# Seven projections of a three-stage transformer block: 512 moving columns in place of 256

## The chip, the cores and the metric

The kernel is one program on one core of one Trainium2 chip. The metric is device time in microseconds of that program, as a median of several executions. One execution was taken by the hardware profiler; all rows below come from it.

## The reference

512 tokens of width 1024 go through two blocks. The first one mixes a gated linear recurrence with a spatial gating unit; the second pools, attends to the 128 best keys of each query, attends to 256 memory tokens and ends in 32 experts. All is float32.

```python
# first block
h = rmsnorm(x, norm_w);  proj = h @ w_in           # ten groups of 1024 columns
y_a = hgrn2(q, f_fwd, f_bwd, i, g)                 # chunks of 64 tokens, both directions
v = layernorm(gelu(v_raw))                         # v_raw = h @ (one group of w_in)
y_b = gelu(u) * mix(w_s, v) * silu(g_b)
x = rmsnorm(x + (sigmoid(m_a) * (y_a @ w_proj_a) + sigmoid(m_b) * (y_b @ w_proj_b)) @ w_out)
# second block
u = rmsnorm(x) @ w_in_2                            # pool, q, k, v, qi (512 each), ki, wi
score[t, s] = sum_h wi[t, h] * relu(qi[t, h] . ki[s]);  sel = top_k(score, 128)
att = softmax(rmsnorm(q) . rmsnorm(k)[sel]) @ v[sel]        # 8 heads of 64, rotary
x = x + concat(pool(u), att) @ w_out_2
q = rmsnorm(rmsnorm(x) @ xattn_wq);  x = x + memory_attention(q) @ xattn_wo   # 4 heads of 128
x = x + moe(rmsnorm(x))                            # 4 groups of 8 experts, width 256
```

## The kernel before

Each float32 product is made of three products in a shorter format: both operands are split into a high part and a low rest, and `mm3` (lines 160 to 163) adds high by high, high by low and low by high in one PSUM bank. Weights come through `load_w` (145 to 158): it loads a matrix block as two raw pieces of 512 KB on SyncE's queue (tag `wr`, two buffers), ScalarE copies the high part (139), and VectorE, or GpSimd where `eng` says so, subtracts for the low part (140). The two parts go into a buffer of the tag `w16`, of which there are two, or into a place given as `dst`.

Two shapes of product are used. With the weights stationary, 512 tokens move (`proj_T`), or with other weights of 512 columns the tokens are stationary. For the seven matrices of this change the tokens are stationary too (`proj_tok`), 128 at a time, and 256 columns of the weight move: a block of 256 columns with its whole contraction of 1024 fills one `w16` buffer, and a PSUM bank of 512 columns holds two token tiles side by side. The seven are the gating unit's value (`wv`, `pv`, in `sg_input`), the first output projection (`wo`, `pwo`, 631 to 648; `load_w4` puts half of its columns in `w16` and half in `wo_H`, `wo_L`), the index queries, keys and queries (`qk_unit`; `pqi`, `pk`, `pq`), the values (`v_unit`, `pvv`), the second output projection (`mix_out`, `pwo2`, in the trace under `pwo` too), and the cross attention's queries (`xq_unit`, `pxq`).

PSUM banks have three tags: `mm` (three banks, all projections), `sm` (three: scores and other small products) and `tp` (two: transposes). `head_norm` (544) normalises each head of a tile: ScalarE squares it out of PSUM, VectorE sums, GpSimd takes the power, VectorE multiplies, again out of PSUM; then `rotate` turns it on VectorE and GpSimd, and TensorE transposes it (`turn`).

`score(i)` (773 to 787) makes the index scores of token tile i: eight products on TensorE (780), a relu on ScalarE (782), a weighted sum on VectorE (784, 786). `topk(i)` (790 to 796) is sixteen rounds of two VectorE instructions on one tile's scores (794, 795). Lists of closures (`pend`, `turns`) and generators decide in which sequence pieces are written; a tile scheduler then sets each engine's sequence, from its own model of time. The expert layer at the end loads 1 MB pieces of gate and up weights on SyncE (1026) into a few buffers.

## Time and profile before

| | us |
|---|---|
| median of three runs | 1312.06 |
| lowest and highest of them | 1311.56, 1314.36 |
| profiled execution, own time | 1309.88 |
| its span on the core | 1308.1 |
| TensorE busy | 1263.4 |
| VectorE, ScalarE, GpSimd busy | 711.3, 490.3, 234.0 |

The mean granted clock of TensorE was 0.997 of full speed. Busy times of matmuls overlap with each other: a row lists a matmul from its start to its modelled end, and the next one starts before that. To see how many fit into a stretch one reads the starts.

### The profile page before, as it was taken

Reading aid. Unit: us, or ns where it says so; the run is one execution under the profiler, and the core shown is the slowest. Engines: PE = TensorE matmul, PEld = TensorE weight load, DVE = VectorE, ACT = ScalarE, POOL = GpSimd, SP = SyncE. Lnnn points to the kernel's source line nnn. Section 1 sums busy time; section 2 is a strip of 40 time slices with the busy share of each in tenths; the row PEclk is TensorE's granted clock in tenths of the full one; section 3 lists DMA queues with packets and bytes.
Section 4 is the critical chain, followed back from the end, with each engine's and each line's share of the span. In section 5 each row is a group of like instructions: output and inputs, shape, how many; then the busy total and the mean of one; then the engine's idle time right before and its main releaser. Section 6 shows DMA issues by size and latency. Waiting matters only on the chain.

```text
span 1308.1 us, 20715 instructions
## 1 busy us (share of the span) xinstructions
PE 1263.4 (97%) x8406; PEld 1000.3 (76%) x8406; DVE 711.3 (54%) x1299; ACT 490.3 (37%) x859; POOL 234.0 (18%) x278
## 2 busy tenths in 40 slices
...
GB/s 191 97 83 53 92 66 66 83 70 75 113 258 95 67 128 94 71 94 98 207 172 106 100 49 73 65 69 146 65 243 336 162 266 416 419 418 418 419 414 226
DMA packets 118085, 218.62 MB, mean 167 GB/s; under 512 B 15280, under 2 KB 94896, under 8 KB 106849
## 3 DMA queue, kind: packets, MB, share of 16 engines
...
## 4 chain that ended last, share of the span: by engine, by line
PE 83%; DVE 6%; DMA 6%; ACT 2%; issue 1%; POOL 1%; ACTq 0%; DVEq 0%; POOLq 0%
PE pgu L1368 8%; PE pl L327 2%; PE pf L162 2%; PE pwo L161 2%; PE pf L163 2%; PE pdn L1392 2%; PE pwo L162 2%; PE pf L161 2%; PE pwo L163 2%; DMA gu<-in_expert_w_gate 2%; PE pdn L1409 1%; PE pq L163 1%; PE ps L780 1%; DMA gu<-in_expert_w_up 1%; PE pq L161 1%; PE pq L162 1%
## 5 line engine op out<-in xcount | busy, mean ns | idle before, releaser
L1368 PE MATMUL pgu<-gu,hgT 128*64 128x512 f32 x512 | 119.0, 595 | 3.7 <-DMA gu<-in_expert_w_up 2.2
L1368 PEld LDWEIGHTS pgu<-gu,hgT 128*64 128x64 f32 x512 | 39.8, 137 | 71.7 <-issue 66.4
L361 ACT ACTIVATE qk<-G 128x512 f32<-128x512 f32 x112 | 69.1, 665 | 51.6 <-DVE G L351 51.6
L1373 DVE SCALAR_TENSOR_TENSOR sh<-sh,grs,pgu 128x256 f32<-128x256 f32 x16 | 7.7, 480 | 105.4 <-ACT sh L1372 105.4
L1372 ACT ACTIVATE sh<-pgu,grs 128x256 f32<-128x256 f32 x16 | 7.6, 474 | 139.2 <-PE pgu L1368 139.2
L348 DVE TENSOR_TENSOR G<-G,T 128x512 f32<-128x512 f32 x56 | 39.2, 701 | 31.4 <-ACT qk L361 28.6
L312 POOL TENSOR_TENSOR T<-T 128x512 f32<-128x512 f32 (+6 forms) x56 | 37.0, 660 | 42.6 <-DVE T L279 38.8
L1343 POOL DMA_INDIRECT hg<-x3d,srci x15 | 15.4, 1025 | 157.5 <-PE thg L1352 109.4
L161 PE MATMUL pi<-wi,hT_h 128*128 128x256 f32 x128 | 37.8, 296 | 3.3 <-ACT wi L139 1.8
L351 DVE TENSOR_TENSOR G<-G,T 128x512 f32<-128x512 f32 x56 | 38.8, 694 | 0.0
L162 PE MATMUL pi<-wi,hT_h 128*128 128x256 f32 x128 | 37.7, 294 | 0.0
L1392 PE MATMUL pdn<-dn,sh 128*64 128x512 f32 x160 | 37.4, 601 | 0.1
L163 PE MATMUL pi<-wi,hT_l 128*128 128x256 f32 x128 | 37.3, 291 | 0.0
L161 PE MATMUL pv<-wv,hT_h 128*128 128x256 f32 x128 | 36.8, 288 | 0.0
L163 PE MATMUL pv<-wv,hT_l 128*128 128x256 f32 x128 | 36.7, 286 | 0.0
L162 PE MATMUL pv<-wv,hT_h 128*128 128x256 f32 x128 | 36.5, 286 | 0.0
L162 PE MATMUL pg<-wga,hT_h 128*128 128x256 f32 x128 | 36.5, 285 | 0.0
L161 PE MATMUL pg<-wga,hT_h 128*128 128x256 f32 x128 | 36.4, 285 | 0.0
L163 PE MATMUL pg<-wga,hT_l 128*128 128x256 f32 x128 | 36.2, 283 | 0.0
L132 POOL TENSOR_SCALAR nm_r<-nm_q 128x1 f32<-128x1 f32 x2 | 2.5, 1254 | 182.5 <-ACT nm_s L200 182.4
L327 PE MATMUL pl<-qk 128*64 128x64 f32 x896 | 34.3, 225 | 0.0
L327 PEld LDWEIGHTS pl<-qk 128*64 128x64 f32 x896 | 29.3, 137 | 6.2 <-issue 2.1
...
## 6 DMA issues: line engine op xcount, KB each, us to landing
...
wo_r<-in_w_out SPq DMA_DIRECT2D x16, 512.0 KB, 3.6
wq_r<-in_w_in SPq DMA_DIRECT2D x12, 512.0 KB, 4.3
dn<-in_expert_w_down SPq DMA_DIRECT2D x10, 512.0 KB, 18.1
wi_r<-in_w_in SPq DMA_DIRECT2D x8, 512.0 KB, 6.5
wfb_r<-in_w_in SPq DMA_DIRECT2D x8, 512.0 KB, 4.3
```

What stands on the lines that cost most here:

```text
L161: nc.tensor.matmul(o, ah, bh, start=first, stop=False)
L162: nc.tensor.matmul(o, ah, bl, start=False, stop=False)
L163: nc.tensor.matmul(o, al, bh, start=False, stop=last)
L312: nc.gpsimd.tensor_tensor(ap_of(T, o, [[n2, 2], [1, n2]]), ap_of(T, a, [[sa, 2], [2, n2]]), ap_of(T, a + 1, [[sa, 2], [2, n2]]), OP.mult)
L327: nc.tensor.matmul(p[64 * j:64 * j + 64, c * 64:c * 64 + 64], kt[:, k0:k0 + 64], qt[:, q0:q0 + 64], start=True, stop=True)
L348: nc.vector.tensor_tensor(ap_of(G, 0, [[512, 2], [2 * m, nb], [1, m]]), ap_of(G, 0, [[512, 2], [2 * m, nb], [1, m]]), ap_of(T, a + 1, [[sa ...
L351: nc.vector.tensor_tensor(ap_of(G, 1024 + m, [[512, 2], [2 * m, nb], [1, m]]), ap_of(G, 1024 + m, [[512, 2], [2 * m, nb], [1, m]]), ap_of( ...
L361: nc.scalar.activation(ap_of(qk, a * 512, [[2 * m, nb], [m, 2], [1, m]]), ap_of(G, a * 512, [[2 * m, nb], [1024 + m, 2], [1, m]]), AF.Copy)
L780: nc.tensor.matmul(p[:, :n], qiT[hs, h // 2, i * 128:(i + 1) * 128], kiT[hs, :n], start=True, stop=True)
L1343: nc.gpsimd.indirect_dma_start(out=h, out_offset=None, in_=x3d, in_offset=bass.IndirectOffsetOnAxis(ap=sidx, axis=0), bounds_check=S - 1, ...
L1368: nc.tensor.matmul(pg[m * a:m * a + m, :], hT_[:, k, m * a:m * a + m], ap_of(gu, k * 256, [[2048, 2], [1, 256]]), start=k == 0, stop=k == 7)
L1392: nc.tensor.matmul(po[m * a:m * a + m, :], hd[:, f, m * a:m * a + m], dn[f][:, hs], start=f == 0, stop=f == 1)
```

## The change

`load_h` loads 512 columns as two halves of the contraction, each in a `w16` buffer of its own (named a and b), so that a raw piece is two blocks of 128 rows by 512 columns and a matrix takes both buffers. `proj_pair` takes two token tiles, a bank each: both with half a, then both with half b, so that every matmul has 512 moving columns. Evictions, residual adds and rotations are 512 wide for one token tile, where they were 256 wide for two. For keys, queries and cross queries `head_norm` first copies the bank to SBUF on ScalarE; the square and the multiply then read the copy. All key projections are written ahead of most score products, and `mix_out` gives way after each token tile and half. In all, 2112 matmuls of 256 columns become 1056 of 512; the other matmuls and the transposes keep their number.

```diff
+    def load_h(src, c0, name, eng=None, dst=(None, None)):
+        return [load_w(src[b * 512:(b + 1) * 512, :], c0, 512, f"{name}{'ab'[b]}", kb=4, eng=eng, dst=dst[b])
+                for b in range(2)]
...
+    def proj_half(o, acts, i, w, b):
+        a, k0 = (acts, 4 * b) if len(acts) == 2 and not isinstance(acts[0], tuple) else (acts[b], 0)
+        for k in range(4):
+            ts = slice(i * 128, (i + 1) * 128)
+            mm3(o, a[0][:, k0 + k, ts], a[1][:, k0 + k, ts], w[b][0][:, k, :], w[b][1][:, k, :],
+                b == 0 and k == 0, b == 1 and k == 3)
+    def proj_pair(acts, ip, w, name, between=None):
+        ps2 = [pmm(f"{name}_{2 * ip + ii}") for ii in range(2)]
+        for b in range(2):
+            for ii in range(2):
+                proj_half(ps2[ii], acts, 2 * ip + ii, w, b)
+            if b == 0 and between:
+                between()
+        return ps2
...
-        for c in range(4):
-            w = load_w(w_in, 6 * D + c * 256, 256, f"wv{c}")
+        for c in range(2):
+            w = load_h(w_in, 6 * D + c * 512, f"wv{c}")
             for ip in range(2):
-                p = pmm(f"pv{c}_{ip}")
-                for ii in range(2):
-                    proj_tok(p[:, ii * 256:(ii + 1) * 256], hT, 2 * ip + ii, w, 0, 256, range(8))
-                nc.scalar.activation(vn[:, 2 * ip:2 * ip + 2, c * 256:(c + 1) * 256],
-                                     p.rearrange("p (i c) -> p i c", i=2), AF.Gelu_apprx_tanh)
+                for ii, p in enumerate(proj_pair(hT, ip, w, f"pv{c}")):
+                    nc.scalar.activation(vn[:, 2 * ip + ii, c * 512:(c + 1) * 512], p, AF.Gelu_apprx_tanh)
...
-    def head_norm(p, name, nh, hd):
+    def head_norm(p, name, nh, hd, copy=False):
 
         t = s4(name)
+        if copy:
+            nc.scalar.activation(t[:, 1, :], p, AF.Copy)
+            p = t[:, 1, :]
...
-        ws = [load_w(src, c * 256, 256, f"{name}{c}", eng=eng) for c in range(2)]
+        first = load_h(src, 0, name, eng=eng)
         hi, lo = a16(name + "_H", F32R), a16(name + "_L", F32R)
-        for c in range(2):
-            ws.append(load_w(src, 512 + c * 256, 256, f"{name}{2 + c}",
-                             dst=(hi[:, :, c * 256:(c + 1) * 256], lo[:, :, c * 256:(c + 1) * 256]), eng=eng))
-        return ws
+        return [first, load_h(src, 512, f"{name}x", eng=eng,
+                              dst=[(hi[:, 4 * b:4 * b + 4, :], lo[:, 4 * b:4 * b + 4, :]) for b in range(2)])]
...
-            for c in range(4):
-                p = pmm(f"pwo{c}_{ip}")
-                for ii in range(2):
-                    proj_tok(p[:, ii * 256:(ii + 1) * 256], mT, 2 * ip + ii, wo[c], 0, 256, range(8))
-                for ii in range(2):
-                    residual(2 * ip + ii, c, 256, p[:, ii * 256:(ii + 1) * 256], xt[ii])
+            for c in range(2):
+                for ii, p in enumerate(proj_pair(mT, ip, wo[c], f"pwo{c}")):
+                    residual(2 * ip + ii, c, 512, p, xt[ii])
...
-                    for c in range(2):
-                        proj_tok(p[:, c * 256:(c + 1) * 256], mT, 2 * ip + ii, wo[2 * c2 + c], 0, 256, range(8))
+                    for b in range(2):
+                        proj_half(p, mT, 2 * ip + ii, wo[c2], b)
...
+    def qk_pair(w, ip, name, tab, norm, dst):
+        for ii, p in enumerate(proj_pair(h2T, ip, w, f"p{name}")):
+            i = 2 * ip + ii
+            if norm:
+                x = head_norm(p, f"{name}n{i}", 8, 64, True)
+            else:
+                x = s4(f"{name}x{i}")
+                nc.scalar.activation(x[:, 1, :], p, AF.Copy)
+            ro = rotate(x, tab, i, 1, 8, f"{name}o{i}", None)
+            def turn(i=i, ro=ro):
+                tp = ptp(f"t{name}{i}")
+                for a in range(4):
+                    nc.tensor.transpose(tp[:, a * 128:(a + 1) * 128], ro[:, a * 128:(a + 1) * 128], ident)
+                nc.scalar.activation(dst[:, :, i * 128:(i + 1) * 128], tp.rearrange("p (a t) -> p a t", a=4), AF.Copy)
+            pend.append(turn)
...
-    wk = load_qk(1024, 0, "k")
-    qk_unit(wk, 0, 0, "k", rk, True, put_k)
-    flush(1)
+    wk = load_h(w_in2, 1024, "wk")
+    qk_pair(wk, 0, "k", rk, True, kT)
+    flush(2)
     score(1)
-    qk_unit(wk, 0, 1, "k", rk, True, put_k)
+    qk_pair(wk, 1, "k", rk, True, kT)
     flush(2)
     score(2)
-    wk = load_qk(1024, 1, "k")
-    for ip in range(2):
-        qk_unit(wk, 1, ip, "k", rk, True, put_k)
...
-        wq = load_qk(512, c, "q")
-        for ip in range(2):
-            qk_unit(wq, c, ip, "q", rq, True, put_q)
-            flush(1)
...
+    wq = load_h(w_in2, 512, "wq")
+    for ip in range(2):
+        qk_pair(wq, ip, "q", rq, True, qT)
+        flush(2)
     topk(1)
-    wv2 = [load_w(w_in2, 1536 + c * 256, 256, f"wvv{c}") for c in range(2)]
-    for c in range(2):
-        v_unit(c, 0)
-        flush()
+    wv2 = load_h(w_in2, 1536, "wvv")
+    def v_out(i, p):
+        nc.scalar.activation(v[:, i, :], p, AF.Copy)
+    for i, p in enumerate(proj_pair(h2T, 0, wv2, "pvv", flush)):
+        v_out(i, p)
...
+        cats = ((pcat[:, 0], pcat[:, 1]), (acat[:, 0], acat[:, 1]))
...
+            for c in range(2):
                 for ii in range(2):
-                    part(p[:, ii * 256:(ii + 1) * 256], 2 * ip + ii, c)
-                for ii in range(2):
-                    residual(2 * ip + ii, c, 256, p[:, ii * 256:(ii + 1) * 256], xt[ii])
-                yield
+                    p = pmm(f"pwo2{c}_{ip}_{ii}")
+                    for b in range(2):
+                        proj_half(p, cats, ii, wo2[c], b)
+                    residual(ii, c, 512, p, xt[ii])
+                    yield
...
+    wxq = load_h(I["xattn_wq_2"][0], 0, "wxq")
+    def xq_pair(ip, between=None):
+        for ii, p in enumerate(proj_pair(h3T, ip, wxq, "pxq", between)):
+            i = 2 * ip + ii
+            qn = head_norm(p, f"xqn{i}", 4, 128, True)[:, 1, :]
...
-    for c in range(2):
-        xq_unit(c, 0)
+    xq_pair(0)
...
+    def first_scores():
+        flush()
         next(first)
+    xq_pair(1, first_scores)
+    next(first)
```

On TensorE, where the first index scores (`ps1_0`) stand, before. `pk1_0` is the second column block of the keys:

```order
L162 MATMUL pk1_0_6933<-wk1_6924,h2T_h_5786 128x256
L163 MATMUL pk1_0_6933<-wk1_6924,h2T_l_5787 128x256
L780 MATMUL ps1_0_6780<-ksc_6361,qk_6359 128x256
L780 MATMUL ps1_1_6785<-ksc_6361,qk_6359 128x256
L780 MATMUL ps1_2_6790<-ksc_6361,qk_6359 128x256
L161 MATMUL pk1_0_6933<-wk1_6924,h2T_h_5786 128x256
```

The same place after; `pk_3` is the last token tile of the keys, with `wkb`, the second half of the contraction:

```order
L166 MATMUL pk_3_6363<-wkb_6216,h2T_h_5594 128x512
L167 MATMUL pk_3_6363<-wkb_6216,h2T_h_5594 128x512
L781 MATMUL ps1_0_6321<-ksc_5973,qk_5971 128x256
L781 MATMUL ps1_1_6326<-ksc_5973,qk_5971 128x256
L781 MATMUL ps1_2_6331<-ksc_5973,qk_5971 128x256
L168 MATMUL pk_3_6363<-wkb_6216,h2T_l_5595 128x512
```

The first scores stood after 117 of the 192 key matmuls, and stand after 92 of the 96 wider ones.

On VectorE, around the first selection round (`MAX m8_1_0`), before. `kn` and `ko` are the normalised and the rotated keys, `sc1` and `ksc` the scores of tiles 1 and 2:

```order
L549 TENSOR_REDUCE kn1_0_q_6984<-kn1_0_6982 128x8
L786 SCALAR_TENSOR_TENSOR sc1_6362<-rl1_6_6812,wi_6672,sc1_6362 128x256
L676 TENSOR_TENSOR ko0_1_a_6878<-kn0_1_6870,ropes_6342 128x512
L786 SCALAR_TENSOR_TENSOR sc1_6362<-rl1_7_6817,wi_6672,sc1_6362 128x256
L787 TENSOR_TENSOR sc1_6362<-sc1_6362,csq_71 128x128
L551 TENSOR_TENSOR kn1_0_6982<-pk1_0_6933,kn1_0_r_6986 128x512
L784 TENSOR_SCALAR ksc_6361<-rl2_0_6885,wi_6672 128x384
L794 MAX m8_1_0_7413<-sc1_6362 128x8
L795 MATCH_REPLACE sc1_6362<-m8_1_0_7413,sc1_6362 128x256
L794 MAX m8_1_1_7416<-sc1_6362 128x8
```

After:

```order
L787 SCALAR_TENSOR_TENSOR sc1_5974<-rl1_3_6338,wi_6188,sc1_5974 128x256
L787 SCALAR_TENSOR_TENSOR sc1_5974<-rl1_4_6343,wi_6188,sc1_5974 128x256
L787 SCALAR_TENSOR_TENSOR sc1_5974<-rl1_5_6348,wi_6188,sc1_5974 128x256
L574 TENSOR_TENSOR kn3_6426<-kn3_6426,kn3_r_6431 128x512
L694 TENSOR_TENSOR ko2_a_6421<-kn2_6412,ropes_5954 128x512
L787 SCALAR_TENSOR_TENSOR sc1_5974<-rl1_6_6353,wi_6188,sc1_5974 128x256
L694 TENSOR_TENSOR ko3_a_6435<-kn3_6426,ropes_5954 128x512
L787 SCALAR_TENSOR_TENSOR sc1_5974<-rl1_7_6358,wi_6188,sc1_5974 128x256
L785 TENSOR_SCALAR ksc_5973<-rl2_0_6454,wi_6188 128x384
L788 TENSOR_TENSOR sc1_5974<-sc1_5974,csq_71 128x128
L795 MAX m8_1_0_6739<-sc1_5974 128x8
L796 MATCH_REPLACE sc1_5974<-m8_1_0_6739,sc1_5974 128x256
```

The multiply and the rotations of the last key tiles moved in front of the first round; before, a sum, a multiply and two rotations of keys, and the split of the second query weights, came behind it.

On ScalarE, in the gating value, before, between the evictions `vn` of the first block; `wv2` is the third column block:

```order
L429 ACTIVATE vn_3280<-pv0_0_3290 128x2x256
L361 ACTIVATE qk6_32_3044<-G6_2638 128x512 x2
L361 ACTIVATE qk6_64_3061<-G6_2638 128x512 x2
L429 ACTIVATE vn_3280<-pv0_1_3340 128x2x256
L139 ACTIVATE wv2_3499<-wv2_r0_3500 128x1024
L139 ACTIVATE wv2_3499<-wv2_r1_3504 128x1024
L369 ACTIVATE G6_2638<-pl6_64_3066 64x4x64 x2
L381 ACTIVATE kt6_3077<-tk6_0_3079 128x384
L381 ACTIVATE kt6_3077<-tk6_1_3084 128x384
```

After; `wv1a` is the first half of the second 512 columns:

```order
L450 ACTIVATE vn_3280<-pv0_1_3300 128x512
L392 ACTIVATE G6_2638<-pl6_64_3066 64x4x64 x2
L404 ACTIVATE kt6_3077<-tk6_0_3079 128x384
L404 ACTIVATE kt6_3077<-tk6_1_3084 128x384
L139 ACTIVATE wv1a_3403<-wv1a_r0_3404 128x1024
L139 ACTIVATE wv1a_3403<-wv1a_r1_3408 128x1024
L411 ACTIVATE sm6_3078<-pkv6_0_3089 128x128
L384 ACTIVATE qk7_1_3146<-G7_2640 128x512 x2
L411 ACTIVATE sm6_3078<-pkv6_1_3096 128x128
L450 ACTIVATE vn_3280<-pv0_2_3351 128x512
```

The next weights' copy stood behind the second eviction of a block, one block ahead; it stands between the evictions of a matrix's first and second token pair, half a matrix ahead.

## Rows read from the trace of the kernel before

**Rows 1.** The page's busy table (share of span, count) and its GB/s by slice.

```profile
PE 1263.4 (97%) x8406; PEld 1000.3 (76%) x8406; DVE 711.3 (54%) x1299; ACT 490.3 (37%) x859; POOL 234.0 (18%) x278
...
GB/s 191 97 83 53 92 66 66 83 70 75 113 258 95 67 128 94 71 94 98 207 172 106 100 49 73 65 69 146 65 243 336 162 266 416 419 418 418 419 414 226
```

**Rows 2.** PE's waits: us in total, times, longest.

```profile
PE thd L1383 <- DVE sh L1373: 13.1, 12, 1.2
...
PE pwo L162 <- DVE wo L140: 0.9, 1, 0.9
```

**Rows 3.** Busy time by stage; x counts instructions, PEclk is the granted clock.

```profile
core 0: us, PE busy (x) PEld busy (x) DVE busy (x) ACT busy (x) POOL busy (x), PEclk, DMA share, GB/s
300.00:366.00 66.00, 66.00 (x713) 63.22 (x712) 41.76 (x72) 33.27 (x57) 4.59 (x8) 1.00 0.39 127
746.00:784.00 38.00, 38.00 (x249) 30.39 (x248) 25.40 (x49) 15.64 (x32) 19.21 (x20) 1.00 0.23 70
784.00:880.00 96.00, 94.69 (x582) 74.94 (x580) 92.22 (x212) 42.46 (x90) 50.17 (x45) 1.00 0.24 71
958.00:1000.00 42.00, 39.81 (x310) 37.56 (x309) 22.99 (x41) 17.06 (x37) 6.67 (x11) 1.00 0.93 331
```

**Rows 4.** PE's timeline in the gating value: start us, listed us, instruction.

```profile
324.61 0.29 PE L161 MATMUL pv<-wv,hT_h 128*128 128x256 f32 x1
...
325.81 0.28 PE L162 MATMUL pv<-wv,hT_h 128*128 128x256 f32 x1
```

**Rows 5.** Tile `pv`: ns shortest/median/longest, first and last start.

```profile
L161 PE MATMUL pv<-wv,hT_h x128: 278/283/387, 301.8 to 364.1; 128*128 128x256 f32 x128
```

**Rows 6.** PE's timeline in a 512-column product, `pmb` and `ppb`.

```profile
619.24 0.39 PE L163 MATMUL pmb<-hT_h,wmb 128*128 128x512 f32 x1
...
621.05 0.39 PE L162 MATMUL ppb<-ybT_l,wpb 128*128 128x512 f32 x1
```

**Rows 7.** Busy time of a long 512-column stretch, columns as in rows 3.

```profile
402.00:502.00 100.00, 100.00 (x443) 82.81 (x442) 34.53 (x39) 31.89 (x37) 0.00 (x0) 1.00 0.34 105
```

**Rows 8.** Timelines of ACT and DVE: one weight split of two raws.

```profile
317.29 1.99 ACT L139 ACTIVATE wv<-wv_r 128x1024 fp32r<-128x1024 f32 x2
...
318.38 2.36 DVE L140 TENSOR_TENSOR wv<-wv_r,wv 128x1024 fp32r<-128x1024 f32 x2 [1.98 <-ACT wv L139]
```

**Rows 9.** The page's DMA issues: count, KB each, median us to landing.

```profile
wq_r<-in_w_in SPq DMA_DIRECT2D x12, 512.0 KB, 4.3
```

**Rows 10.** ACT's timeline in the first output projection: first and last split.

```profile
661.47 1.06 ACT L139 ACTIVATE wo<-wo_r 128x1024 fp32r<-128x1024 f32 x1 [1.20 <-DMA wo_r<-in_w_out]
...
683.25 1.06 ACT L139 ACTIVATE wo_H<-wo_r 128x1024 fp32r<-128x1024 f32 x1 [1.77 <-DMA wo_r<-in_w_out]
```

**Rows 11.** Timelines of PE and DVE: first key, first score, first selection.

```profile
745.39 0.40 PE L161 MATMUL pk<-wk,h2T_h 128*128 128x256 f32 x2
...
761.10 1.13 PE L780 MATMUL ps<-ksc,qk 64*128 64x256 f32 x6
...
774.86 0.42 DVE L794 MAX8 m<-sc 128x8 f32<-128x256 f32 x1
```

**Rows 12.** Tile `kn`: square and sum, ns shortest/median/longest.

```profile
L547 ACT ACTIVATE kn<-pk x4: 591/596/597, 751.8 to 783.7; 128x512 f32<-128x512 f32 x4
L549 DVE TENSOR_REDUCE kn_q<-kn x4: 668/678/678, 753.6 to 784.7; 128x8 f32<-128x512 f32 x4
```

**Rows 13.** Line 795, the selection's replacement: first and last start.

```profile
L795 DVE MATCH_REPLACE8 ksc<-m,ksc x32: 534/609/679, 812.8 to 876.1; 128x384 f32<-128x384 f32 x16, 128x512 f32<-128x512 f32 x16
```

**Rows 14.** The chain of waits near the end: start us, us, what.

```profile
1240.13 21.16 DMA gu<-in_expert_w_gate
1261.31 18.08 DMA gu<-in_expert_w_up
```

**Rows 15.** Timelines of PE and SyncE where the expert layer begins.

```profile
1058.96 3.63 PE L1368 MATMUL pgu<-gu,hgT 128*64 128x512 f32 x16
...
1066.41 0.33 SPq L1026 DMA_DIRECT2D gu<-in_expert_w_gate  x1
```

89 lines of the change are left out of this document (19 added, 70 removed).

## The prediction

> **What bounds the kernel now.** I read the page's busy table first, then TensorE's waits, then the busy time by stage. TensorE (PE) is busy for 97% of the span, every other engine for 54% or less [rows 1]. Its waits are short: the largest is 13.1 us in twelve pieces, on the expert layer's `sh`; of those in front of the seven matrices the largest is 0.9 us, once, for a weight split [rows 2]. By stage, those that hold the matrices have PE busy throughout at the start (66.00 of 66 us for the gating value), 94.69 of 96 in the attention and 39.81 of 42 at the cross queries, at a granted clock of 1.00 [rows 3], which is the 2.4 GHz level. So up to about 1059 us the end is set by the number of matmuls times their spacing, with one stretch, 784 to 880 us, in which VectorE (DVE) is nearly full too, with 92.22 of 96 us [rows 3].
>
> After that the expert layer is fed by weights. The last 1 MB pieces take 21.16 and 18.08 us to land and stand in the chain of waits [rows 14], and the load rate is flat at 414 to 419 GB/s in the last full slices [rows 1]. But this stream doesn't run on its own clock: the gate and up loads issued from 1066.41 us on need buffers that PE's first expert matmuls, from 1058.96 us, give back [rows 15]. If all before comes earlier, the stream starts earlier by as much, and a gain made before 1059 us reaches the end. Only the prefetch around slices 30 and 31 is at the engine's own pace, at 243 and 336 GB/s [rows 1], under the flat rate.
>
> **The main term.** The change replaces 2112 matmuls of 256 moving columns by 1056 of 512: 384 for the gating value `pv`, 768 for the two output projections `pwo`, 192 each for `pqi`, `pk`, `pq`, `pvv`, `pxq` (each of their rows on lines 161 to 163 stands for a third, as `pv`'s x128 [rows 5]). What counts is the distance from start to start, not the 283 or 389 ns that a row lists, for these overlap. At 256 columns ten steps, 324.61 to 325.81 us, take 1.20 us: 120 ns each [rows 4]. At 512 columns eight steps, 619.24 to 621.05 us, take 1.81 us: 226 ns [rows 6]. The stretch from 402 to 502 us, filled with such products, holds 443 matmuls in 100.00 us: 226 ns again [rows 7]. Two halves cost 240 ns, one whole 226: 14 ns less, within about 2 ns either way since the starts are given to 10 ns. I take 13, since single steps of 119.5 ns fit the rows as well: 1056 x 13 ns = **13.7 us**, bounds 12.7 to 15.8. By matrix: `pv` 2.5, first `pwo` 2.5, second 2.5, the five others 1.25 each.
>
> Read as a line through both widths, the rows give 106 ns per 256 columns and 13 to 14 ns for every matmul whatever its width; the change buys one such fixed part per merged pair. The Trainium skill, "TensorE: Matmul & The Clock Gate", section "Back-to-back issue gap", gives 262 and 518 cycles for these widths, that is 6 cycles (2.5 ns) of overhead. By it merging two matmuls would give 2.5 ns, and the sum 1056 x 2.5 = 2.6 us, nearly nothing. The rows do not agree (120 and 226 ns against its 109 and 216), so I go by the rows; it stands beside rival 1.
>
> **Weights in two halves.** Each load of 512 columns and half the contraction fills one of the two `w16` slots, so one matrix holds both. Before, the next block of 256 columns was split while the last was used, with 96 matmuls (11.5 us) to hide in. Now the next matrix's first half can be split only when the current one's last pair is done with half a: 24 matmuls x 226 ns = 5.4 us before its end. The split of two raw pieces takes from 317.29 us on ScalarE (ACT) to 320.74 on DVE (318.38 + 2.36): 3.45 us [rows 8]. The raws of the first half are loaded ahead into the two raw buffers. Slack 1.9 us. The second half's raws start when the first are used up: about 2.3 us, then 4.3 us of load [rows 9] and 2.3 of split end at 8.9 us, and PE wants them at 5.4 + 5.4 = 10.8. Slack 1.9 us again, so I price it at nothing; what hides it is the last half-matrix, and other work (chunks of the linear attention, scores, transposes) between. What ACT or DVE is late beyond 1.9 us shows in full. On SyncE's queue the pieces keep their places, but for the first one of the cross queries, now one place ahead of two residual loads: these wait with it for a raw buffer, at most one split (2.3 us), and are needed only at a later residual add: 0.
>
> At the first output projection the weights come one by one anyway: eight pieces are split from 661.47 to 683.25 us, 3.11 us apart [rows 10]; with 12 matmuls per piece and token pair PE eats one in 2.71 us instead of 2.88, and the second token pair's work fills in. I charge 0.5 us, bounds 0 to 1.5 (nearest row: the 0.9 us wait there now [rows 2]).
>
> **Banks.** A pair takes two of the three `mm` banks. The next pair's first 12 matmuls run in the third for 2.7 us, while an eviction takes 0.60 us on ACT [rows 12] or about as long on DVE; 0. Evictions and rotations handle as many elements as before in equally many 512-wide instructions; 0. The output projection's 256-wide residual adds become fewer, a saving on an engine that isn't the bound there.
>
> **Keys, queries, cross queries copied first.** Twelve more ACT copies of 128x512, bounded by the square of the same tile, 0.60 us [rows 12]: 7.2 us on an engine busy for 15.64 of 38 us there [rows 3], off the path. Each makes its normalised tile 0.6 us later; scores, later projections and the transposes of other tiles stand between, so 0. The bank is free earlier, by reduce, power and multiply; a gain from that would need PE to wait for banks, and the largest wait ahead of these matrices is the one for a weight [rows 2]. GpSimd's powers and rotations keep number, size and sequence.
>
> **Score and selection.** Here order moves, on PE and DVE (the two pieces ahead). Before, the first score product started at 761.10 us, 15.7 after the first key matmul at 745.39 [rows 11]. Now 92 of the 96 key matmuls stand ahead of it: 92 x 0.226 = 20.8 us and the same transposes, so about 7 later; the first selection round, which began at 774.86 us [rows 11], comes some 4 later because the scores then follow more closely (my estimate from the two orders). Against this, key work on DVE that stood behind that round (one reduce, one multiply and two rotations, some 0.7 us each, and the split of the next query weights, 2 x 1.2 [rows 8, 12]) now stands ahead of it, where DVE had time: it was busy for 25.40 of 38 us from 746 to 784 [rows 3]. That is about 5 us of relief. So the last selection, at 876.1 us [rows 13], should come about 1 us earlier, while PE's own work before it shrinks by `pk`, `pq`, `pvv` (3.7 us) and a first part of `pwo` (1.2). The difference, up to 4 us, becomes PE waiting for masks and probabilities. Bounds of the loss: 0 (PE finds other projections to fill in, as it does there now [rows 3]) to 8 (DVE not relieved: the 4 us delay on top of the 4). I take 3, near the middle, because the fill-in work is still there.
>
> **Sum.** 13.7 - 0.5 - 3.0 = 10.2 us. Fewer changes between 64-wide and 128-wide work (the rows of key, query and pooling projections are less cut up) may add 0 to 2; not counted. Of the profiled execution's 1309.88 us (span 1308.1 and 1.78 around it) that leaves 1299.7. The median of the three runs is 1312.06, 2.2 above the profiled one, and the forecast is for a median: 1312.06 - 10.2 = **1302 us**.
>
> **Rivals.**
> 1. *The change doesn't do what it says.* In these places the spacing follows the columns, and one matmul of 512 takes as long as two of 256, 240 ns: gain 0, and no later loss since nothing comes earlier: 1312. For it: the pairs alternate banks, weights and tokens as no product does now. Against: 512-column products with a weight load of the same size (128 rows by 128 columns) already run at 226 [rows 6, 7]. Chance 0.05. The Trainium skill's rule above ("TensorE: Matmul & The Clock Gate", "Back-to-back issue gap") would leave 2.6 us of gain here, 1309.5; the rows speak against it.
> 2. *Selection takes it back.* DVE late by 4 us and full, so 8 us lost, 13.7 - 0.5 - 8 = 5.2: 1307. For it: DVE's 92 of 96 us. Against: relief of 5 us. Chance 0.2.
> 3. *Slower: the two slots.* With both taken, each of nine successions (`pv` to its second half, to the merge weights, into and out of the first output projection, then qi, k, q, v, the second output projection) waits for its split. For it: the cover falls from 11.5 to 5.4 us. Against: 1.9 us slack and filler work. If the splits queue behind other ACT and DVE work for 3.7 us in the mean, each waits 1.8: 9 x 1.8 = 16 us, +6 with the loss above: 1318. It is slower from 1.1 us of wait for each (10.2 / 9). Chance 0.15.
> 4. *More than the sum.* The relief holds, switches give 2, no loss: 13.7 + 2 = 15.7: 1296. Chance 0.15.
> The forecast itself, 1299 to 1305: 0.45.
>
> **Numbers.** Faster by over 0.2% (2.6 us, about what a measurement here can tell from no change) are the forecast, rival 4 and rival 2, less 0.02 for mixtures with late splits: 0.78. Same: rival 1 and the mild cases of rival 3, 0.05 + 0.03 = 0.08. Slower: the rest of rival 3 and the mixtures, 0.14. The range runs from below rival 4 (the 15.8 bound and 2 us for changes would be 1294) to rival 1, 1313; it leaves out what is slower and a few hundredths of rival 1.
>
> **What would show it.** Right: 512-column steps of 226 ns in all seven matrices; PE's busy time about 13 us less; the expert layer's first matmul some 10 us earlier than 1058.96 and the same distance from there to the end. Rival 1: steps above 235 ns. Rival 2: PE waits on DVE's mask, probabilities or selection, some 8 us between 800 and 880. Rival 3: PE waits on lines 139 and 140 of `wv1a`, `wma0`, `wqa`, `wvva`, `wxqa` above 1 us each. I am wrong as a whole if the expert layer's weights do not move with its first matmul.

## The result: 11 us slower, and the profile after

The changed kernel takes 1323.73 us (median of six runs, 1321.09 to 1324.57), the kernel before 1312.91 in the same job: a ratio of 1.0078, interval 1.0062 to 1.0094. 10 us less were forecast. The profiled execution took 1324.57 us, with a span of 1322.8 and a mean granted clock of 0.989 (0.997 before).

The page of the changed kernel, busy time, against [rows 1]. TensorE (PE) is busy for 8 us less in a span that is 15 us longer:

```profile
PE 1255.7 (95%) x7350; PEld 942.1 (71%) x7350; DVE 716.4 (54%) x1291; ACT 498.2 (38%) x871; POOL 233.1 (18%) x278
```

PE's timeline in the cross queries after: start, listed time, instruction. From 983.03 to 985.53 us stand eleven steps of 227 ns, the spacing of [rows 6]; two halves took 240 [rows 4]. In the other changed products the median step is 0.23 us too, to the 10 ns in which starts are given:

```profile
983.03 0.40 PE L168 MATMUL pxq<-wxqb,h3T_l 128*128 128x512 f32 x1
...
985.53 0.39 PE L168 MATMUL pxq<-wxqa,h3T_l 128*128 128x512 f32 x1
```

PE's waits after: total, times, longest. In [rows 2] `thd` had 13.1 us with a longest of 1.2, and the largest wait ahead of a changed matrix was 0.9:

```profile
PE thd L1373 <- DVE sh L1363: 22.9, 12, 10.3
...
PE ppm L837 <- issue: 5.2, 1, 5.2
PE txq L1059 <- DVE xqn L574: 3.1, 1, 3.1
...
PE pwo L166 <- ACT wo_H L139: 1.9, 1, 1.9
```

Busy time by stage, the kernel before first, then after; columns as in rows 3. What PE's busy time lacks to the length is its idle time:

```profile
18.00:660.00 642.00, 640.16 (x4480) 560.97 (x4480) 363.99 (x531) 281.74 (x426) 66.69 (x102) 1.00 0.32 102
660.00:784.00 124.00, 123.01 (x934) 112.91 (x933) 73.90 (x108) 48.50 (x80) 40.72 (x48) 1.00 0.33 104
784.00:960.00 176.00, 173.66 (x1199) 139.39 (x1198) 125.69 (x293) 87.11 (x194) 68.91 (x58) 1.00 0.27 85
960.00:1060.00 100.00, 96.54 (x754) 87.34 (x754) 63.59 (x223) 35.23 (x91) 13.25 (x26) 1.00 0.68 251
```

```profile
18.00:660.00 642.00, 636.41 (x4279) 548.71 (x4278) 364.04 (x532) 281.41 (x425) 67.43 (x103) 1.00 0.32 102
660.00:784.00 124.00, 120.60 (x569) 96.88 (x570) 66.52 (x81) 50.58 (x80) 43.42 (x51) 0.97 0.36 114
784.00:960.00 176.00, 168.88 (x808) 112.83 (x807) 132.71 (x311) 91.05 (x201) 65.28 (x56) 0.99 0.24 77
960.00:1060.00 100.00, 94.05 (x588) 80.57 (x587) 63.13 (x215) 36.83 (x94) 14.12 (x26) 0.97 0.68 254
```

Idle time up to 1060 us rose from 8.6 us (1.8 + 1.0 + 2.3 + 3.5) to 22.1 (5.6 + 3.4 + 7.1 + 6.0): 13.4 more. On top of it PE ran below full clock for a while behind three of the waits, which it never did before in this stretch (windows of the changed kernel, columns as above; the clock stands third from the end, 0.50 is the 1.2 GHz level):

```profile
680.00:684.00 4.00, 1.83 (x4) 1.33 (x5) 2.61 (x4) 2.11 (x2) 0.00 (x0) 0.76 0.31 96
684.00:688.00 4.00, 4.00 (x11) 3.03 (x11) 1.49 (x2) 1.06 (x1) 0.00 (x0) 0.50 0.79 246
688.00:692.00 4.00, 4.00 (x17) 3.29 (x16) 0.68 (x1) 0.00 (x0) 0.00 (x0) 0.89 0.46 140
```

Busy time times the missing clock, summed over all such windows of 4 us (these, 856 to 864 and 996 to 1008), makes 7.2 us. So up to the expert layer the bill is -13.7 (spacing) + 13.4 (idle) + 7.2 (clock) = +6.9; the first expert matmul came 4.2 us later, counted from the kernel's first transposes in both traces. The other 2.7 were not traced to a place; the less cut-up rows, which the prediction left uncounted at 0 to 2 us, may be part of them, but no run shows it. The remaining 10 us of the loss stand at the very end. There VectorE (DVE) waits 10.84 us for data of another engine, and PE behind it 10.29 (timelines of DVE and PE after):

```profile
1294.62 3.39 DVE L1456 TENSOR_TENSOR fx<-fx,yt 128x1024 f32<-128x1024 f32 x1 [10.84 <-POOL yt L1454]
1297.93 5.04 DVE L1406 TENSOR_SCALAR put<-csq,srcf 128x128 fp32r<-128x128 f32 x4
1302.89 0.47 DVE L1363 SCALAR_TENSOR_TENSOR sh<-sh,grs,pgu 128x256 f32<-128x256 f32 x1
...
1303.42 0.70 PE L1373 MATMUL thd<-csq,sh 128*128 128x128 f32 x2 [10.29 <-DVE sh L1363]
```

`sh` of the last expert block is what PE needs next; ahead of it in DVE's queue stands an addition of the final sum, which waits for `yt`, read back from `yd`. In the kernel before, `sh` stood ahead of that addition (DVE's timeline there):

```profile
1288.00 0.48 DVE L1373 SCALAR_TENSOR_TENSOR sh<-sh,grs,pgu 128x256 f32<-128x256 f32 x1 [8.50 <-ACT sh L1372]
1289.56 3.38 DVE L1466 TENSOR_TENSOR fx<-fx,yt 128x1024 f32<-128x1024 f32 x1 [1.08 <-POOL yt L1464]
```

The chain of waits of the changed kernel shows that the load was what ended last, 15.72 us:

```profile
1276.26 15.72 DMA yt<-yd
1292.23 2.36 POOL yt L1454
1294.62 3.39 DVE fx L1456
```

The selection itself, line 795 before and 796 after. The first line is the kernel before's, for the scores `sc`; its second one is in [rows 13]. The selection begins 14.6 us later and ends 13.8 later.

```profile
L795 DVE MATCH_REPLACE8 sc<-m,sc x16: 402/408/411, 775.4 to 811.8; 128x256 f32<-128x256 f32 x16
...
L796 DVE MATCH_REPLACE8 ksc<-m,ksc x32: 531/608/678, 820.5 to 889.9; 128x384 f32<-128x384 f32 x16, 128x512 f32<-128x512 f32 x16
L796 DVE MATCH_REPLACE8 sc<-m,sc x16: 398/409/412, 790.0 to 820.1; 128x256 f32<-128x256 f32 x16
```

Of the 14.6 us, 3.1 come from ahead: the first key matmul stands at 748.54 us, where it stood at 745.39 [rows 11]. The first score product follows it by 22.7 us instead of 15.7, and the first selection round follows that by 18.2 instead of 13.8 (timelines of PE and DVE after):

```profile
771.25 1.13 PE L781 MATMUL ps<-ksc,qk 64*128 64x256 f32 x6
...
789.42 0.43 DVE L795 MAX8 m<-sc 128x8 f32<-128x256 f32 x1
```

### The profile page after: what moved, and what is told of

It reads as the page before. It is cut to its first block, busy times and chain, and to the rows that moved or that the text cites. A ratio compares the mean times of both kernels' runs of the same rounds, so it can differ in the third digit from the quotient of the medians.

```text
span 1322.8 us, 18584 instructions
## 1 busy us (share of the span) xinstructions
PE 1255.7 (95%) x7350; PEld 942.1 (71%) x7350; DVE 716.4 (54%) x1291; ACT 498.2 (38%) x871; POOL 233.1 (18%) x278
## 5 line engine op out<-in xcount | busy, mean ns | idle before, releaser
L1373 PE MATMUL thd<-csq,sh 128*128 128x128 f32 x32 | 7.8, 326 | 22.9 <-DVE sh L1363 22.9
L1373 PEld LDWEIGHTS thd<-csq,sh 128*128 128x128 f32 x32 | 5.3, 203 | 33.3 <-DVE sh L1363 33.0
L166 PEld LDWEIGHTS pi<-wi,hT_h 128*128 128x128 f32 x128 | 24.8, 194 | 5.4 <-ACT wi L139 2.6
```

What stands on the lines that cost most here:

```text
L166: nc.tensor.matmul(o, ah, bh, start=first, stop=False)
```

## Experiments: the end of the kernel

Theory 1: the 10 us at the end come from the tile scheduler, which by its own model put one `fx` addition ahead of `sh` in DVE's queue; the change has no instruction there. Rival: the last block's data come late. To test it, the additions were tied by data behind `sh` and behind results of the last block, in both kernels ("guarded"):

```diff
-            V_.tensor_tensor(fx[:, i, :], fx[:, i, :], ys[0][:, i, :], OP.add)
+            V_.tensor_scalar(one, late, 0.0, 1.0, OP.mult, OP.add)
+            V_.scalar_tensor_tensor(fx[:, i, :], ys[0][:, i, :], one, fx[:, i, :], OP.mult, OP.add)
```

`g_after` is the changed kernel so guarded, `g_before` the kernel before. `g_before_bad` is the guarded kernel before in which the same trick forces one addition ahead of the last `sh`.

> The kernel before, with the order at the very end fixed by data: each of the four adds of the gathered rows to the output on VectorE (line 1466 of before) takes a factor one that is made from the last expert pair's hidden tile or from a finished output block, so none of them can stand ahead of the last hidden tile. In the kernel before they already stood behind it. Theory 1 (one such add, standing ahead of the last hidden tile on VectorE's in-order queue, costs the changed kernel some 10 us at the end): no difference from before, within 0.2%, 1310 to 1315 us. Theory 2 (the changed kernel's tail is longer because the expert weights come later or slower): the same 1310 to 1315. This run is the control for the other three.

> The kernel before with the reverse forced: the gate of the last expert pair takes its value through the first add of gathered rows, so that this add stands ahead of the last hidden tile on VectorE, as it does in the changed kernel. Theory 1: 7 to 10 us longer than before, 1320 to 1323 us, with TensorE waiting 7 to 10 us for the last hidden tile. Theory 2: that order is harmless since the rows are there in time, under 2 us longer, 1312 to 1315 us.

> The changed kernel with the order at the end fixed as in the control. Theory 1: the 10 us at the end go, 1313 to 1315 us, so that what is left against before is at most 0.2%; TensorE's wait for the last hidden tile falls from 10.3 us to about 1. Theory 2: the stream of expert weights sets the end, 1321 to 1324 us as the changed kernel.

Measured, against the kernel before on the same chip (1310.29): `g_before` 1312.69, ratio 1.0017 (1.0007 to 1.0027); `g_before_bad` 1321.31, 1.0079 (1.0058 to 1.0100); `g_after` 1313.78, 1.0021 (1.0008 to 1.0034). PE's waits for `thd`, in this order:

```profile
PE thd L1383 <- DVE sh L1373: 13.1, 12, 1.2
```

```profile
PE thd L1383 <- DVE sh L1373: 20.4, 12, 7.7
```

```profile
PE thd L1373 <- DVE sh L1363: 13.1, 12, 1.2
```

So this order alone costs the kernel before 8.6 us (1321.31 less 1312.69). The changed kernel stood 10.8 us above the kernel before (each difference within one job); guarded it stands 3.5 above it and 1.1 above the guarded one, since the guard itself costs the kernel before 2.4. That settles the loss, not the missing gain: guarded against guarded the two are level, where 10 us of gain were computed. The stream of expert weights did move with its first matmul, as the prediction wanted it: from there to the end of the span it is 249.1 us before, 251.3 in `g_before` and 250.4 in `g_after`. All kernels below are guarded.

## Experiments: where the 10 us of gain went, place by place

Each of these undoes or relieves one place of `g_after`. "Earlier" and "later" count from the kernel's first transposes, against `g_before`. Each trace is one execution, and in some of them (`g_after_ln`, `g_after_top`) a lower clock near the start shifts all that follows by 1.7 us; a distance between two places of one trace is not touched by that.

**The landing of `wpa`.** The gating value does end 4.6 us earlier, but the next product, `ppa`, keeps only 1.0 of that to its end. Theory D: its weights land late, since a 4 MB fill of `yd` with zeros is on the DMA engines just then. Theory C: the LayerNorm behind the gating value is late. `g_after_zero` moves the fill into the second block; `g_after_ln` leaves out the second pass of the LayerNorm.

```diff
-    nc.scalar.dma_start(yd.rearrange("(i p) d -> p i d", p=128), ap_of(zero, 0, [[0, 8], [1, D]]))
...
     nwx = row_bc(...)
+    nc.scalar.dma_start(yd.rearrange("(i p) d -> p i d", p=128), ap_of(zero, 0, [[0, 8], [1, D]]))
```

> The changed kernel with the end fixed, and without the second pass of the layer norm of the gating value (line 462: four VectorE instructions of 1.2 us, which scale by the deviation and add the bias; this part of the computation is left out). Theory C (the 4.2 us that the gating value's matmuls save are given back because VectorE's layer norm and splits right behind it, 357 to 381 us, do not get shorter): the last product of the first merge (ppa) ends 3 to 4 us earlier than with the end fixed alone, relative to TensorE's first instruction, and the whole gets 2 to 4 us shorter, about 1310. Theory D (the gain is lost for another reason, such as the weights of the merge): ppa's end stays within 1 us, no shorter.

> The guarded changed kernel (its DVE order at the end set as before), with one more edit: the 4 MB zero fill of `yd`, which goes out on ACT's queue during the linear attention, is written behind the residual of the second block instead. In the guarded changed kernel the transfers share the chip's load path with that fill at 407 to 420 GB/s between about 350 and 377 us, and the raw pieces of `wpa` take 10.9 us to land. Theory D (the gating value's gain is taken back because `wpa` lands late): the raws land in about 5 us, the split of `wpa` comes 4 to 6 us earlier, the first `ppa` product starts 3 to 4 us earlier than in the guarded changed kernel, and the end moves by 2 to 4 us less if nothing later waits: about 1310. Rival D2 (the norm chain, not the weight, sets the first `ppa` product): `ppa` starts within 0.7 us of where it does, end unchanged at about 1314. A third way: the fill, moved, collides with the weights of the cross attention, and the gain at `ppa` is lost behind 900 us.

`g_after_ln`: 1322.14, ratio 1.0078 (1.0055 to 1.0101): no gain at `ppa` (0.1 us earlier; from the end of the gating value to that of `ppa` 0.5 us less than in `g_after`), theory C falls; `ppa` now waits 1.7 us for the split of `wpa`. The first expert matmul comes 7.3 us later than in `g_after`, and 5.8 of that are lower clock (9.7 us against 3.9, up to the expert layer). `g_after_zero`: PE's idle time there is gone (the window 340 to 380 us in `g_after`, then in `g_after_zero`), and the split of `wpa` moves from 376.57 to 365.66 us; from issue to landing the raws take 4.7 us instead of 12.3.

```profile
340.00:380.00 40.00, 37.56 (x256) 31.56 (x253) 30.62 (x48) 18.18 (x29) 8.18 (x8) 1.00 0.62 224
```

```profile
340.00:380.00 40.00, 40.00 (x274) 34.20 (x271) 30.86 (x47) 17.37 (x28) 7.28 (x7) 1.00 0.43 145
...
884.00:888.00 4.00, 4.00 (x9) 2.29 (x10) 1.19 (x6) 3.49 (x11) 3.37 (x2) 0.55 0.99 351
888.00:892.00 4.00, 4.00 (x15) 2.41 (x13) 0.00 (x0) 1.01 (x4) 0.37 (x1) 0.59 1.03 412
```

`ppa` now ends 4.4 us earlier, so the fill is what took the gain at that place. Whether by the landing alone is not shown: with the fill gone the scheduler also puts the split of `wpa` 11 us earlier on ScalarE, and `ppa` ahead of work that it stood behind. The time is 1312.99, ratio 1.0016 (1.0006 to 1.0027). The fill now stands at 880 to 900 us, with waits and the lower clock (last two rows), and by the end of the second output projection 1.0 of the 4.4 us is left. That looks like the third way of the expectation, but the run doesn't show it: `g_after_top` below, which has no fill there, loses 9.9 us in the same stage, where this run loses 10.7.

**The pieces of `wo`.** Theory A: two raw buffers pace the eight pieces at 3.1 us, while PE, at 512 columns, eats one in 2.7. `g_after_wor` puts every second pair of pieces into spare buffers. `g_after_wofill` orders the work of all four token tiles for the first 512 columns ahead of the other columns.

```diff
-            raw = sb.tile([128, k2, n], F32, name=f"{name}_r{b}", tag="wr", bufs=2)
+            if raws is None:
+                raw = sb.tile([128, k2, n], F32, name=f"{name}_r{b}", tag="wr", bufs=2)
+            else:
+                raw = raws[:, b * 1024:(b + 1) * 1024].rearrange("p (k n) -> p k n", k=k2)
```

> The guarded changed kernel, in which the second halves' raw pieces of the first output projection's weights go into two spare 8 KB buffers, so that four raw pieces are in flight and not two. Theory A (two raw buffers, each held for about 4 us of load, 1.06 on ACT and 1.22 on DVE, pace the pieces at 3.1 us or more while PE eats one in 2.72): PE's waits for `wo` and `wo_H` in the stretch 655 to 690 us fall from about 5 us to under 2, the projection ends about 3 us earlier, the end comes 2 to 3 us earlier: about 1311. Rival A2 (DMA's own rate paces the pieces): the gaps stay within 1 us of what they are, end about 1314.

> The changed kernel with the end fixed, and the first output projection in another order: the first 512 columns for all four token tiles, then the second 512, so that each weight half serves twice as many matmuls before the next is needed. Theory A (the 5.3 us of gaps on TensorE between 659 and 683 us of the changed kernel come from waiting for weights that are loaded at 3.1 to 3.3 us per piece, with the third bank's work standing behind the waiting matmuls): gaps there fall to about 1 us, the low clock right after them goes too, 5 to 7 us shorter than the run with the end fixed alone, about 1307 us. Theory B (the gaps come from banks or from the split on ScalarE and VectorE): no shorter than that run, 1313 to 1315.

Both remove the wait for `wo_H` and both end later: 1323.80, ratio 1.0105 (1.0086 to 1.0124), and 1321.90, 1.0088 (1.0067 to 1.0110). Their first expert matmuls come 9.8 and 8.9 us later than in `g_after`; 5.9 and 5.2 of that are lower clock, the rest is waits and what was not traced. In the first the free buffers let SyncE issue the new loads early, ahead of weights that are needed sooner (SyncE's timeline, then PE's wait); in the second the transposes of the normed tiles wait instead.

```profile
623.68 2.20 SPq L158 DMA_DIRECT2D wo_r<-in_w_out  x4
628.04 3.86 SPq L158 DMA_DIRECT2D wpb_r<-in_w_proj_b  x2
...
PE ppb L169 <- ACT wpb L139: 3.8, 1, 3.8
```

```profile
PE tp_h2T_h L216 <- DVE h2T_l L140: 3.1, 1, 3.1
```

**The cross queries.** Theory G: the wide form makes each tile's chain (copy, square, sum, power, multiply, transpose) longer where nothing stands between. `g_after_xq` takes the old form, `g_after_xqnc` keeps the width and leaves the copy away (`head_norm` without its last argument).

> The changed kernel with the end fixed, and the cross attention's query projection as before the change (256 columns, two blocks, no copy first). Theory G (the copy and the two token tiles of a pair that end together make the last normalisation late, so that TensorE waits 3.1 us for the transposes of the queries and runs at half clock for some microseconds): that wait goes, the stretch from the last query matmul to the last score of the cross attention is some 5 us shorter, against 1.3 us more of matmuls: 3 to 4 us shorter, about 1310. Rival H (what follows, the values' products, waits anyway): under 1.5 us shorter.

> The changed kernel with the end fixed, and the 512-column query projection of the cross attention kept, but without its copy first: square and multiply read the bank. Theory G1 (the copy, two more instructions on ScalarE's in-order queue behind the exponentials and the weight split, makes the chain late): the 3.1 us wait for the queries falls to about 1, as large a gain as with the old projection, 3 to 5 us. Theory G2 (the pair, whose two tiles end together, does it): the wait stays within 1 us of 3.1, no gain.

`g_after_xq`: 1311.75, ratio 1.0001 (0.9989 to 1.0013). The wait of 3.1 us for `txq` and the lower clock behind it are gone, and the end of the router's lists comes 4.2 us earlier instead of 0.9. `g_after_xqnc`: 1313.30, 1.0011 (1.0000 to 1.0022). The wait has moved on, and it is shorter:

```profile
PE pxo L1099 <- DVE xpe L1093: 2.5, 1, 2.5
```

From the first cross query to the end of the router's lists it is 97.3 us in `g_after`, 95.7 without the copy, 94.9 in the old form and 94.9 in `g_before`. So of the 2.4 us that the change loses here 1.6 are the copy's; the width loses the other 0.8, and the 1.25 that its spacing should have brought. Each figure is from one execution (1.3, 1.5 and 0 us of lower clock in the first three), and the time as a whole doesn't tell the two forms with 512 columns apart.

**The first pooling product.** Theory E: `ppm` waits 5 us for DVE's sums, which stand in the queue behind selection rounds (PE's waits put this one down to "issue" and name no engine). `g_after_topk` leaves out 8 of the 16 rounds of tile 1 (`range(8 if i == 1 else 16)`).

> The changed kernel with the end fixed, and with 8 instead of 16 selection rounds for token tile 1 (this part of the selection is left out; 8 rounds of about 0.92 us on VectorE, 7.4 us). Theory E (the gain of keys, queries and values is given back because VectorE is the bound from the scores to the pooling's last product, and TensorE then waits 5.0 us for the pooled tiles on line 837, and runs at half clock after that): the wait there falls under 1 us, the low clock at 852 to 864 us goes, and the kernel gets 5 to 8 us shorter, 1306 to 1309. Theory F (TensorE's wait is for GpSimd or for weights): wait unchanged, under 2 us shorter.

1313.54, ratio 1.0019 (1.0006 to 1.0032). The wait for `ppm` is gone and another one on DVE stands in its place; about 1 us is won for 6.6 us of DVE's work:

```profile
PE tP L885 <- DVE PT L889: 3.3, 2, 2.9
```

## Experiments: the places together

`g_after_best` joins the late fill, the spare buffers and the old cross queries; `g_before_best` is the kernel before with the first two.

> The guarded changed kernel with three edits together: the late zero fill, four raw pieces in flight at the first output projection, and the cross queries `pxq` in their old form (256 columns, no copy ahead). If the 10 us that the narrower spacing saves are taken back at exactly these three places and at the selection (about 3 us, left as it is), the gains add: 3 to 4 at `ppa`, 2 to 3 at `wo`, 3 at the cross queries, some of it lost again behind the selection: about 1306 (1303 to 1309), 4 to 8 us under the unchanged kernel with the same late fill and raw pieces. If instead each gain is taken back by the next wait, it ends at 1311 to 1314, level with that one.

> Control: the kernel before with the guarded order at the end and the same two edits, the late zero fill and four raw pieces in flight at the first output projection. Its 256-column stages had nearly no waits there (0.9 us for a weight of `wo`), so both theories expect the time of the guarded kernel before, 1311 to 1313, at most 1 us less. If it gains as much as the changed kernel does with these edits, the edits act for themselves, and nothing is shown of the wider matmuls.

1311.17, ratio 0.9995 (0.9985 to 1.0005), and 1320.19, 1.0064 (1.0049 to 1.0080). They are 9 us apart, where 4 to 8 were expected, but this is no clean ground: the spare buffers' loads make `ppb` wait in both, and the kernel before, expected unchanged, ends 8.3 us above the kernel without edits, where `g_before` ended 2.4 above it. So the two transfers were put where nothing waits for them: the fill in four parts of 1 MB during the second gate, the spare raws fetched there on GpSimd's queue (`g_after_top`, with the old cross queries, and `g_before_top`). `g_after_top2` takes in addition the old form for index queries, keys and queries.

```diff
+        for a in range(2):
+            nc.gpsimd.tensor_scalar(zero[:, a * 512:(a + 1) * 512], m_, 0.0, 0.0, OP.mult, OP.add)
+        nc.scalar.dma_start(yd[c * 256:(c + 1) * 256, :].rearrange("(i p) d -> p i d", p=128), ...)
+        if c < 2:
+            wo_fetch(c, m_)
```

> The guarded changed kernel, cross queries in their old form, and the two transfers out of the way where nothing waits for them: the zero fill of `yd` in four parts of 1 MB during the second gate (`pmb`, `ppb`), and the second halves' raw pieces of the first output projection's weights fetched one by one on GpSimd's queue in the same stretch. If the narrower spacing is worth about 10 us and what took it back are the landing of `wpa`, the pieces of `wo`, the cross queries and the selection, it ends 7 to 10 us under the unchanged kernel with the same two edits and at 1302 to 1306. If each gain is taken back by whatever waits next, the two end within 2 us of each other.

> Control: the guarded kernel before with the same two edits (zero fill in four parts during the second gate, every second pair of raw pieces of the first output projection fetched early). It had little to gain there (0.9 us for `wo`), so 1311 to 1313 is expected by both theories. If it loses some 7 us as with the four pieces on SyncE's queue, these edits are no clean ground for the comparison.

> As the first of these, but indexer queries, keys and queries also in their old form and order (256 columns, keys not copied first, the score products between the keys as before); wide are the gating value, both output projections and the values. Theory S (in the score and selection stage VectorE sets the pace, so that 3 x 1.25 us of spacing won there for keys and queries are not won at the end, and the later scores cost some on top): ends level with the first or up to 3 us earlier: about 1301 to 1305. Rival S2 (their spacing counts in full): about 3.7 us later than the first, 1306 to 1309.

`g_after_top` 1311.61, ratio 1.0000 (0.9987 to 1.0013); `g_before_top` 1313.74, 1.0017 (1.0004 to 1.0030), so the ground is clean; `g_after_top2` 1312.83, 1.0012 (0.9999 to 1.0024), 1.2 us later than `g_after_top`, between its two theories and nearer to S. The pair is 2.1 us apart, against 12.5 computed (13.7 less 1.25 for the cross queries). The traces say where that is lost: the changed kernel is 6.1 us ahead of its control at the single index key `pki`, and the merges behind that (`pk`, `pq`, `pvv`, second `pwo`) are worth 6.25 more by the spacing; but at the start of the last matmul of the second output projection it is only 2.5 ahead. 9.9 us vanish between (PE's timelines, control first; the first transposes start at 7.99 and 8.15 us):

```profile
742.35 0.48 PE L165 MATMUL pki<-h2T_h,wki 128*72 128x512 f32 x1
...
966.30 0.28 PE L167 MATMUL pwo<-wo_H,acat 128*128 128x256 f32 x1
```

```profile
736.40 0.47 PE L170 MATMUL pki<-h2T_h,wki 128*72 128x512 f32 x1
...
963.94 0.48 PE L172 MATMUL pwo<-wo_H,acat 128*128 128x512 f32 x1
```

Stage 784 to 960 us, control first, then `g_after_top` with two of its windows:

```profile
784.00:960.00 176.00, 173.67 (x1190) 138.65 (x1190) 126.25 (x298) 87.22 (x194) 68.96 (x58) 1.00 0.26 81
```

```profile
784.00:960.00 176.00, 167.88 (x783) 111.44 (x782) 125.60 (x303) 89.06 (x196) 60.20 (x52) 0.97 0.25 78
...
852.00:856.00 4.00, 3.14 (x7) 1.02 (x7) 3.72 (x10) 2.58 (x6) 3.75 (x3) 0.54 0.01 4
856.00:860.00 4.00, 4.00 (x14) 2.91 (x13) 3.46 (x11) 1.57 (x6) 3.07 (x3) 0.61 0.46 131
```

Idle time is 5.8 us more (8.1 against 2.3), and 4.7 us go by lower clock (busy time times the missing clock, 852 to 860 and 884 to 892 us): 10.5 in all. From 852 to 860 us, where PE waits and then runs at the lower clock, DVE is busy for 3.72 and 3.46 of 4 us. The wait is the one for `ppm`: GpSimd (POOL) makes its operand and waits for DVE itself, and projections (`ppu`) whose weights were split by 847 us stand behind `ppm` in PE's queue:

```profile
849.34 1.04 POOL L849 TENSOR_TENSOR pool<-pool 128x510 f32<-128x510 f32 x1 [2.58 <-DVE pool L848]
...
852.86 2.05 PE L858 MATMUL ppm<-pool,pw 128*128 128x512 f32 x2 [5.28 <-issue]
...
857.01 0.80 PE L170 MATMUL ppu<-h2T_h,wpu 128*128 128x512 f32 x1
```

The later selection is not what takes the gain alone. In `g_after_top2`, where the replacements run from 775.1 to 876.1 us as in the kernel before, PE is 3.3 us ahead of the control at `pki`, has 3.75 more to win by the spacing, and starts the last matmul of the second output projection 0.2 behind it. Of the 7.2 us lost there idle time and lower clock make up 3.9; the rest was not traced. What PE brings to the stage matters little: 3.0 us behind (`after`), and 1.3, 5.5 and 6.1 ahead (`g_after`, `g_after_zero`, `g_after_top`) at `pki` become 0.5 behind, and 3.5, 1.1 and 2.5 ahead at that last matmul.

## Experiments: is VectorE the wall?

Theory W: from its first selection round to its last DVE needs some 100 us whatever PE does (first to last replacement: 775.4 to 876.1 before, 790.0 to 889.9 after), so what PE saves ahead and in it turns into waits there. Rival V: the waits have other causes. `g_after_half` and `g_before_half` are the last pair with 8 rounds a tile instead of 16; `g_after_pool` leaves nothing out but splits the value weights on GpSimd.

```diff
-        for rd in range(16):
+        for rd in range(8):
```

> The changed kernel with the three edits of the run before the last batch's control (guarded end, old cross queries, zero fill and raw pieces out of the way), and 8 instead of 16 selection rounds for each of the tiles 1 to 3, so that some 27 us of VectorE's work in the selection are left out: the result is another one. Theory W (VectorE sets the pace from the first selection round to the last, and TensorE's gain of the keys, queries, values and of all before turns there into waits and into half clock behind them): with the rounds gone TensorE's idle time from 784 to 960 us falls from 8.1 to under 4 us, no stretch of half clock is left there, and the kernel ends 8 to 11 us under the unchanged one with the same cut. Rival V (the gain is used up by waits elsewhere, the selection is no wall): the distance of the two stays at the 2 us that it has with all rounds.

> Control: the unchanged kernel with the guarded end, the same two edits on transfers and the same cut of the selection to 8 rounds a tile. TensorE idled only 2.3 us from 784 to 960 us with all rounds, so both theories expect little from the cut: 1310 to 1313. If it gains as much as the changed kernel does, VectorE was the bound there before the change too.

> The changed kernel with guarded end, old cross queries, zero fill and raw pieces out of the way, and the split of the value weights on GpSimd instead of VectorE (4 x 1.2 us off the engine that is full there, 4 x 2.4 us onto one that is busy for half of it). Nothing is left out. Theory W: TensorE's wait for the first pooling product falls from 5.3 to about 1 us and the half clock behind it goes with it; of 5 us of relief 2 to 5 reach the end: 1307 to 1310, under the kernel before. Rival: as with 8 rounds less for one tile, the wait moves to the next operation of VectorE, and under 1.5 us come back.

`g_after_half` 1306.23, ratio 0.9944 (0.9924 to 0.9965); `g_before_half` 1315.00, 1.0022 (1.0009 to 1.0036). They are 8.8 us apart; with all rounds it was 2.1. (What is missing to 12.5 was lost earlier: `g_after_half` is only 2.9 us ahead at `pki`, and its `ppb` waits 1.8 us for `wpb`, with 1.7 of lower clock behind it.) The control gained nothing by the cut, so DVE did not bind before the change. The stage, control first, then changed:

```profile
784.00:960.00 176.00, 175.03 (x1189) 138.74 (x1188) 99.61 (x226) 87.48 (x194) 69.88 (x58) 1.00 0.26 81
```

```profile
784.00:960.00 176.00, 173.46 (x838) 116.59 (x837) 106.56 (x242) 93.42 (x204) 61.44 (x54) 1.00 0.28 88
```

Idle time is 2.5 us instead of 8.1, the clock stays at 1.00, and from `pki` to the end of the second output projection the changed kernel gains 6.5 us on its control (2.9 to 9.4 ahead), where the spacing says 6.25. Theory W holds for this cut: with some 27 us of DVE's work gone, the spacing comes through. (The result is then another one, and the scheduler's orders move with the cut; that a new order alone brings the gain was not tried.)

`g_after_pool`: 1315.23, ratio 1.0030 (1.0014 to 1.0045), a miss. Taking 5 us off DVE moved the wait from `ppm` on to the next thing that DVE makes, as its rival said:

```profile
PE tP L906 <- DVE PT L910: 4.0, 1, 4.0
```

The last replacement came 4.3 us earlier than in `g_after_top` (878.1 against 882.4), yet from `pki` to the last matmul of the second output projection PE took as long (227.6 and 227.5 us). So it is not the end of the selection by itself that PE waits for. How much DVE work must go, and which of its results bind, is open between the 5 us of this run and the 27 of the other.

No version with the whole computation was found that beats the kernel before by more than the interval.

## Why the prediction was wrong

**The spacing was right.** 227 ns against two times 120 is 13 ns a pair, 13.7 us in all. The pair with the cut selection returns 6.5 us for a computed 6.25 (480 merged pairs) where nothing else binds. By an estimate from the rule of the Trainium skill that was weighed there ("TensorE: Matmul & The Clock Gate", section "Back-to-back issue gap", which gives it for a matmul by itself) that would have been 480 x 2.5 ns = 1.2 us; the runs speak for the rows. PE's busy time, named as a sign with 13 us less, fell by 7.7: work at the lower clock counts as busy for longer, by 7.2 us up to the expert layer.

**Where the sum failed.** How much each stage got longer or shorter (us, from the traces; each row runs from the mark above it to its own, the first one from the kernel's first transposes):

| up to | forecast | before to after | `g_before` to `g_after` |
|---|---|---|---|
| last `pv` | -2.5 | -4.2 | -4.7 |
| last `ppa` | 0 | +4.0 | +3.7 |
| last `ppb` | 0 | 0.0 | 0.0 |
| `pki` (first output projection, index queries) | -3.25 | +3.2 | -0.4 |
| last `pwo` of the second output projection (selection) | -3.25 | -2.6 | -2.2 |
| first expert matmul (cross queries) | -1.25 | +3.7 | +2.6 |
| end of the span | 0 | +10.4 | -0.9 |

The terms that failed are those at nothing or next to it: the stage behind the gating value (4.0), the pieces of `wo` (charged 0.5, lost 7.0 with the clock), the cross queries (5.0) and the end.

**Score and selection: the size by luck, the mechanism wrong.** The sum charged 3.0 us with bounds of 0 to 8, and the changed kernel lost 3.7 there (6.25 less 2.6). The estimate had the first round 4 us later and the last 1 us earlier, thanks to relief on DVE. In the trace the first came 14.6 later and the last 13.8; in `g_after`, where PE was 1.3 us ahead at `pki`, 10.0 and 9.8 (785.8 to 886.6 against 775.8 to 876.8 in `g_before`). The first score product was put rightly, 7.0 us later behind the first key. The next step failed: from it to the first round the estimate took off some 3 us, and 4.4 were added. There was no relief: the key work and weight splits that by the two orders now stand ahead of the first round are DVE's own, and only changed places; from the first round to the last replacement it is 100.5 us after and 101.2 before. The loss stayed small because PE came to the stage with no lead; with a lead of 6.1 us (`g_after_top`) it was 9.9, and the forecast had PE come with one of 5.75. In that stage waits made up 5.8 us and the lower clock behind them 4.7; for the clock the sum had no term. The warning stood in the prediction's own row, 92.22 of 96 us busy [rows 3]: of 12.4 us that were ahead or to be won in the stage, that pair kept 2.5, which is less than DVE's slack of 3.8. The sentence that "PE finds other projections to fill in" failed, because in PE's queue the waiting product stands ahead of them.

**What was priced at nothing.** The gating value's gain was carried to the end without asking what waits next. It was `wpa`, whose raws shared the DMA engines with the zero fill: in `g_after` 3.6 of 4.6 us were lost there. In the kernel before the two transfers met as well, but PE came by 4 us later. The `wo` pieces were charged 0.5 (0 to 1.5); idle time from 660 to 784 us rose by 2.4 and the clock took 2.9 more in this profile. The fill-in work of the second token pair, which was to cover that, stands behind `wo_H` on PE. The copies for the cross queries were taken to be hidden by other work: there was too little, and PE waited 3.1 us; without the copy the stage is 1.6 us shorter. Of the steps on weights in halves, the slack of 1.9 us held inside the gating value. The banks showed no wait.

**The end was not looked at.** The prediction followed the weight stream and said that what comes earlier ends earlier. It did not compare DVE's order at the end, where the diff changes nothing, and there the scheduler had moved one addition: 10 us. The two orders of DVE, laid side by side at the end, would have shown the place; the landing of `yt<-yd`, 13.8 to 15.0 us in the kernel before, would have hinted at the price.

**The rivals.** Rival 2 (the selection takes it back) is what happened to the gain where the places ahead were relieved; in the changed kernel itself the selection took 3.7 us of 13.7. Rival 3 named waits at each succession of weights; they came at two of them, and the time was beyond its 1318 for another reason, the end.
